# Gated linear attention in a two-layer hybrid block: the second head pair's projections get buffers of their own and are written ahead of its decays, and two modulation groups are written behind both pairs

## The chip, the cores and the metric

The kernel runs on one core of a Trainium2 chip. The metric is device time in microseconds (us) of one execution, median of three runs. Engines: PE is TensorE (matrix products), DVE is VectorE, ACT is ScalarE, POOL is GpSimd, SP is the engine whose queue issues the DMA transfers. PSUM is the small memory that PE writes to, here eight banks of 128 x 512 floats.

## The reference, cut to what matters

Two layers of a transformer block over 256 latent and 256 context tokens of width 1024. Each layer is modulated by six rows that come from a timestep vector (adaLN), has three parallel token mixers (grouped attention, gated linear attention, neighbourhood attention) and a mixture of experts. The part at hand is the gated linear attention (GLA) with 4 heads, which the kernel takes as 2 pairs of heads, and the modulation's product.

```
mod = silu(c) @ w_mod + b_mod              # 6 rows of 1024; a "group" here is 2 of the 6
z = h @ w_in + b_in                        # q, k (64 a head), v, r (128 a head), a (gate rank 16)
log_g = log_sigmoid(a @ w_gate + b_gate) / 16          # one for each direction: the decays
# per head and direction, over the tokens:
S_t = diag(exp(log_g_t)) S_{t-1} + k_t^T v_t
o_t = q_t S_t
o = rms_norm(o_forward + o_backward) * norm_g * silu(r)
```

## The kernel before

**Order of the work.** The program is written as plain Python that traces one instruction after the other. A scheduler then orders each engine's instructions by the order of tracing, by when it reckons that their inputs are ready, and by when buffers come free. What it decides is a fixed list for each engine: on the chip each engine works its list off in order, and an instruction that waits holds up all that stand behind it on its engine. The same holds for the transfers on SP's queue.

**One pair (`gla_pair`, L636).** `gla_decay` makes the decays: two small products z (L619), then on ACT and DVE absolute value, exponential, logarithm and running sums into the tile gc (C in the code). `projT` (L384) projects q and k, transposed, into the PSUM tiles pT, from which they are copied into the tile qTkT; `projM` (L393) projects V and the gate r of the four 128-token tiles into four PSUM tiles pM, from which V, r and rn are made. Then comes a chain. EK and EQ are the keys and queries times their decays. In two halves kET (PE transpose), kE (copy), dS (PE, one product a chunk) and a copy of dS. Eight levels of block products G (PE), each of which needs YX, made on DVE, POOL and ACT, and each of which is copied by mask into Sd on DVE; then Sd is copied to S on POOL. Then o (PE) for each token tile and each head of the pair, the RMS norm of o on ACT and DVE, and oT (PE transposes) with `put_o`, which casts oT to o0 on ACT and subtracts on DVE. In layer 0 a pair has four token tiles, in layer 1 two, as the context's output isn't needed there.

**Projections.** A matrix product in full precision is three products of parts (`mm3`: high by high, low by high, high by low; L380 to L382). So each weight piece of 128 x 1024 floats is loaded into a tile of the pool raw (4 buffers, 512 KB each) and split into whi (ACT, L291) and wlo (DVE, L292), which have 3 buffers each. A pair takes six pieces: one for q, one for k, four for V and r. One piece of q or k is 24 products, one of V and r is 24 too (6 for each of the four token tiles): 144 in all.

**Modulation (`modulation`, L471).** One group is 16 weight tiles (wmod) of 512 KB, which come from the pool raw as well, and two products of PE by each of them (L495), which the trace records as four. All 16 add up in one PSUM tile (mod), which is copied (L500) and transposed (modT). Layer 0 does group 1 behind pair 0 and group 2 behind pair 1; layer 1 does group 1 in its opening, with other buffers, and group 2 behind pair 1.

**PSUM.** The eight banks go by two names of four each. pT, pM, z, mod, modT and aT share one four; kET, dS, G, o and oT share the other.

**Pools.** g4 (10 buffers of 4 KB a partition in layer 0) holds ge, gc, qTkT, V, rn, EQ, EK, dS and S of a pair; o4 has 8 buffers, of which the output o0 of this mixer takes four.

Of the kernel before, what the change touches and what calls it, by code (L numbers as in the profile page):

```python
# [249 lines left out]
class _Prog:  # L250
# [385 lines left out]
    def gla_pair(self, l, pair, T):  # L636
        nc, mm = self.nc, self.nc.tensor.matmul
        nq = 128 * T
        C, end = self.gla_decay(pair)
        p = self.projT(l, ("Bq", pair), nq)  # L640
        qk = self.t([128, 2, 512], "g4", name="qTkT")
        qT, kT = qk[:, 0], qk[:, 1]
        nc.vector.tensor_scalar(qT[:, :nq], p[:, :nq], self.bt[:, BT["Bq", pair]:BT["Bq", pair] + 1], 0.125, op0=ALU.add, op1=ALU.mult)
        p = self.projT(l, ("Bk", pair), 512)
        nc.scalar.activation(kT, p, AF.Identity, bias=self.bt[:, BT["Bk", pair]:BT["Bk", pair] + 1])  # L645
        brow = self.bias_row(l, 768 + 512 * pair, 512)
        V = self.t([128, 4, 256], "g4", name="V")
        rn = self.t([128, 4, 256], "g4", name="rn")
        ps = self.projM(l, [("Bvr", pair, i) for i in range(4)], 2, 512, range(4), {t: 256 for t in range(T, 4)})
        for t in range(4):  # L650
            nc.vector.tensor_tensor(V[:, t], ps[t][:, :256], brow[:, :256], op=ALU.add)
            if t < T:
                r, th = self.t([128, 256], "u1", name="r"), self.t([128, 256], "u1", name="th")
                nc.vector.tensor_tensor(r, ps[t][:, 256:], brow[:, 256:], op=ALU.add)
                nc.scalar.activation(th, r, AF.Tanh, scale=0.5)
                nc.vector.scalar_tensor_tensor(r, th, 1.0, r, op0=ALU.add, op1=ALU.mult)
                nc.gpsimd.tensor_tensor(rn[:, t].rearrange("p (h e) -> p h e", h=2), r.rearrange("p (h e) -> p h e", h=2),
                                        self.gn[:, None, :].to_broadcast([128, 2, 128]), op=ALU.mult)

        F, B = C[:, 0], C[:, 1]  # L660
        EQ, EK = self.t([128, 2, 512], "g4", name="EQ"), self.t([128, 2, 512], "g4", name="EK")
# [15 lines left out]
        for i in (1, 0):  # L677
# [8 lines left out]
            for t in range(2):  # L686
                for d in range(2):
                    o = 256 * t + 128 * d
                    for h in range(2):
                        mm(pd[64 * h:64 * h + 64, o:o + 128], kE[:, t, d, 64 * h:64 * h + 64], V[:, 2 * i + t, 128 * h:128 * h + 128],  # L690
                           start=True, stop=True)
# [58 lines left out]
        for t in range(T):  # L750
            ts = slice(128 * t, 128 * t + 128)
            for h in range(2):
                hs = slice(64 * h, 64 * h + 64)
                inter = [(0, Sf), (1, Sb)]
                inter = [(i, s[t]) for i, s in inter if t in s]
                mm(pos[h][:, ts], S[:, t, h], V[:, t, 128 * h:128 * h + 128], start=True, stop=not inter)
                for n, (i, s) in enumerate(inter):
# [79 lines left out]
    def attention(self, l, T):  # L837
        nc, mm = self.nc, self.nc.tensor.matmul
        brow = self.bias_row(l, 0, 768)
        V = self.t([128, 4, 128], "u2", name="AV")  # L840
        kTs = self.t([128, 2, 512], "g4", F32R, "kTs")
# [3 lines left out]
        for t in range(4):  # L845
            z = self.t([128, 256], "u1", name="zkv")
            nc.vector.tensor_tensor(z, ps[t][:, :256], brow[:, 512:768], op=ALU.add)
            nc.gpsimd.tensor_copy(V[:, t], z[:, 128:])
            o = self.norm_rope(l, z[:, :128], 2, 1, t)
# [35 lines left out]
        def scores(qT, kv, pair):  # L885
            def emit(o, i, ks):
                for h in range(2):
                    q = qT[i][:, 2 * pair + h]
                    mm(o[h], q, kTs[:, kv, ks], start=True, stop=False)
                    mm(o[h], q, kTl[:, kv, ks], start=False, stop=True)  # L890
            return emit

        units = []
        for lat in ((True, False) if T == 4 else (True,)):
            qT = {}
            for pair in range(4):
                kv = pair // 2
                vs = slice(64 * kv, 64 * kv + 64)
                units.append(dict(lat=lat, prep=[lambda i=i, q=qT, t=i if lat else i + 2: q.__setitem__(i, prep(t)) for i in range(2)] if pair == 0 else [],
                                  scores=scores(qT, kv, pair), v=lambda k, h, vs=vs: V[:, k, vs], nb=None, out=(1, pair)))  # L900
        self.attend(units)
# [713 lines left out]
    def run(self):  # L1615
        nc, a = self.nc, self.a
        self.md, self.mT, self.mT2, self.nraw = {}, {}, {}, {}
        self.setup()
        self.rp = self.ctx.enter_context(self.tc.tile_pool(name="rp", bufs=1))
        self.x2 = [self.dr.tile([128, 1024], F32, name=f"x2_{t}") for t in range(2)]  # L1620
        src = [a["x"][0:128], a["x"][128:256], a["cx"][0:128], a["cx"][128:256]]
        xs = None
        for l in range(NL):
            T = 4 if l == 0 else 2
            if l == 0:
                left, right = self.mixers(0)
                xs = []
                for t in range(4):
                    x = self.t([128, 1024], "o4", name="x")
                    nc.sync.dma_start(x, src[t])  # L1630
                    xs.append(x)
                self.vectors(l)
                self.setup2()
                self.modulation(0, [0], ["h4"] * 8 + ["y4"] * 4 + ["raw"] * 4)
            self.norm_T(l, xs)
            if l:
                self.modulation(1, [1], "o4", "b2", "tmod")
            if l:
                self.vectors(l)
            self.oT, self.y = {}, []  # L1640
            self.gla_gates(l)
            self.open_o(0)
            for p in range(2):
                self.gla_pair(l, p, T)
                if l == 0 or p == 1:
                    self.modulation(l, [1 + p])
            self.held, self.nw, self.spare = {}, 0, []
            us = groups(l)[0][0]
            self.load(l, us, 0, range(4), most=PRE[l], after=self.aT)
            self.open_o(1)  # L1650
            self.attention(l, T)
            self.merge(l, 0, T)
            self.open_o(2)
            self.neighbourhood(l, T)
            self.merge(l, 1, T)
            self.merge(l, 2, T)
            self.out_norm(l, T, src if l == 0 else self.x2)
            left.close()
            left = self.open("eg", "left", [("ew", 6)])
            if l == 0:  # L1660
                self.modulation(1, [0], "ew")
            self.load(l, us, 0, range(4), most=6)
            self.route(l, T)
            if not LAST[l]:
                self.h2_done(l, T - 1)
            if l:

                self.spare = [[self.t([128, 1024], ("whi", "wlo")[v] if tag == "wx" else tag, name="ew") for v in range(2)] for tag in ("raw", "h4", "h4", "wx")]
            right.close()
            right = self.open("ep", "right", [("ewb", RNG[l]), ("e8", 2), ("g2", T // 2), ("oh", 2), ("o1", 2), ("e2", NE2[l]), *([("c2", NC2[l])] if l else []), ("ct", NCT[l]), ("row", 2)])  # L1670
            self.experts(l, T)
            if l:
                lgb = self.final_loads(l)
            self.overflow(l, T)
            if l == 0:
                right.close()
                left.close()
                self.pre.close()
                left, right = self.mixers(1)
                lgb = self.final_loads(l)  # L1680
            xs = self.final_norm(l, T, lgb)
        right.close()
        left.close()
        self.pre.close()
# [27 lines left out]
```

## Time and profile before

| what | value |
|---|---|
| median of three runs | 2152.49 us (2150.43 to 2153.63) |
| the profiled execution | 2150.77 us, span 2148.9 us |
| PE busy | 1973.0 us, 92% of the span |
| DVE, ACT, POOL busy | 45%, 26%, 13% |
| mean granted clock of PE | .969 |
| moved by DMA | 562.41 MB, mean 262 GB/s |

The span is the stretch from the first to the last instruction of the profiled execution; the 1.9 us beside it are start and end. Stages on the time axis: layer 0 opens until 52 us, its two GLA pairs take until about 216, its other mixers until about 700, its experts until about 1190 (at 370 to 420 GB/s). Layer 1's GLA pairs lie between about 1245 and 1370, its experts from about 1650 to the end. Numbers of times below are us from the start of the span.

### The profile page before, as it was taken

The page shows a single profiled execution, that of the slowest core. Times are in us where ns is not written, and L with a number is a line of the kernel's source. Part 1 is how long each engine was busy: PE and PEld are TensorE (multiplying, and loading weights), DVE is VectorE, ACT ScalarE, POOL GpSimd, SP SyncE. Part 2 cuts the span into 40 slices and gives each one's busy share as a digit, 9 for nine tenths or more (in the row PEclk, how much of TensorE's full clock was granted, in tenths as well). Part 3 has the DMA queues.
Part 4 walks back from the last instruction along what each step waited for, and adds up shares of the span by engine and source line. Part 5 has one row for each costly group of instructions (what it writes and reads, how often), then busy time and mean ns, then how long its engine had stood idle before and what let it go on. Part 6 is the DMA issues. An engine that isn't in the chain of part 4 may idle for free. (4 is left out here: it accounts for less than half of the span.)

```text
span 2148.9 us, 28075 instructions
## 1 busy us (share of the span) xinstructions
PE 1973.0 (92%) x10749; PEld 1179.0 (55%) x10749; DVE 964.7 (45%) x2236; ACT 561.5 (26%) x992; POOL 277.5 (13%) x268
## 2 busy tenths in 40 slices
PE   6999999999998898989899598999996999999995
PEld 2676777767885353445253176887795433333331
DVE  4676765554487131222022766776658222221113
ACT  3453344443333000000010254444452111100000
POOL 1322100011100010111011222100020001000000
PEclk9999999999999999999999798999997999999998
DMA  8436222333328999999998723642466999999995
GB/s 300 160 118 220 69 69 70 94 99 120 99 91 321 400 420 420 372 385 420 420 369 367 276 84 116 197 127 85 140 210 253 401 421 422 422 422 422 421 422 224
DMA packets 113987, 562.41 MB, mean 262 GB/s; under 512 B 13302, under 2 KB 14838, under 8 KB 72120
## 3 DMA queue, kind: packets, MB, share of 16 engines
q1 hardware_dynamic: 113272, 558.85, 67.7%
q8 instruction: 87, 1.43, 0.3%
q10 hardware_dynamic: 576, 1.70, 0.2%
q14 instruction: 52, 0.43, 0.1%
HBM read 557.36 MB, written 3.15 MB: 261 GB/s over the span
## 5 line engine op out<-in xcount | busy, mean ns | idle before, releaser
L1507 PE MATMUL h<-ew,XT 128*64 128x512 f32 (+2 forms) x2048 | 479.0, 616 | 39.6 <-DMA ew<-in_ew_dram 39.5
L1507 PEld LDWEIGHTS h<-ew,XT 128*64 128x64 f32 (+2 forms) x2048 | 147.3, 136 | 325.7 <-issue 251.0
L1415 PE MATMUL Y<-ew,aT 128*64 128x512 f32 (+2 forms) x1024 | 250.4, 598 | 10.2 <-DMA ew<-in_ew_dram 7.8
L292 DVE TENSOR_TENSOR wlo<-raw,whi 128x1024 fp32r<-128x1024 f32 (+1 forms) x140 | 179.1, 1279 | 138.0 <-ACT whi L291 136.9
L1433 POOL TENSOR_TENSOR x<-x,ct 128x512 f32<-128x512 f32 x82 | 104.9, 1306 | 996.9 <-DVE ct L1432 873.7
L380 PE MATMUL pT<-hThi,whi 128*128 128x512 f32 (+1 forms) x576 | 204.0, 354 | 2.2 <-DVE zq L869 1.4
L291 ACT CAST whi<-raw 128x1024 fp32r<-128x1024 f32 (+1 forms) x140 | 145.4, 1039 | 223.4 <-PE pT L381 123.8
L382 PE MATMUL pT<-hThi,wlo 128*128 128x512 f32 (+1 forms) x576 | 203.2, 353 | 0.2 <-DVE wlo L292 0.2
L381 PE MATMUL pT<-hTlo,whi 128*128 128x512 f32 (+1 forms) x576 | 202.9, 352 | 0.0
L1404 DVE SCALAR_TENSOR_TENSOR act<-h,s,sl 128x512 f32<-128x512 f32 x30 | 22.5, 751 | 317.6 <-PE h L1507 263.9
L806 ACT CAST Yh<-Y 128x512 fp32r<-128x512 f32 x60 | 35.2, 586 | 467.7 <-PE Y L1415 467.7
L1415 PEld LDWEIGHTS Y<-ew,aT 128*64 128x64 f32 (+2 forms) x1024 | 75.5, 133 | 149.2 <-issue 123.8
L807 DVE TENSOR_TENSOR Yl<-Y,Yh 128x512 fp32r<-128x512 f32 x60 | 41.4, 690 | 252.8 <-ACT Yh L806 249.7
L380 PEld LDWEIGHTS pT<-hThi,whi 128*128 128x128 f32 x576 | 110.7, 192 | 23.8 <-issue 6.0
L382 PEld LDWEIGHTS pT<-hThi,wlo 128*128 128x128 f32 x576 | 110.7, 192 | 16.1 <-issue 2.6
L381 PEld LDWEIGHTS pT<-hTlo,whi 128*128 128x128 f32 x576 | 110.7, 192 | 14.3 <-issue 1.9
L380 PE MATMUL pM<-whi,hThi 128*128 128x512 f32 (+1 forms) x304 | 110.7, 369 | 3.6 <-ACT qTkT L645 1.9
L381 PE MATMUL pM<-wlo,hThi 128*128 128x512 f32 (+1 forms) x304 | 110.9, 365 | 0.0
L382 PE MATMUL pM<-whi,hTlo 128*128 128x512 f32 (+1 forms) x304 | 110.1, 364 | 0.0
L495 PE MATMUL mod<-wmod,sT 128*32 128x512 f32 x320 | 75.2, 636 | 22.5 <-DVE s L341 14.1
L1408 ACT COPY aT<-aT 128x512 f32<-128x512 f32 x30 | 17.6, 585 | 294.4 <-PE aT L1407 294.4
L1384 PE MATMUL XT<-OH,h2hi 128*128 128x256 f32 x352 | 88.6, 289 | 0.2 <-DVE OH L1362 0.2
(364 smaller groups left out, 3088.5 us busy)
## 6 DMA issues: line engine op xcount, KB each, us to landing
ew<-in_ew_dram SPq DMA_DIRECT2D x326, 1024.0 KB, 13.6
raw<-in_w_dram SPq DMA_DIRECT2D x145, 512.0 KB, 3.7
ew<-in_ew_dram SPq DMA_DIRECT2D x116, 512.0 KB, 13.5
wmod<-in_wmod_dram SPq DMA_DIRECT2D x96, 512.0 KB, 6.4
nb<-in_nb_dram SPq DMA_DIRECT2D x32, 256.0 KB, 3.8
g<-md SPq DMA_DIRECT2D x12, 256.0 KB, 7.3
row<-in_ln_dram SPq DMA_DIRECT2D x4, 512.0 KB, 5.3
lgb<-in_ln_dram SPq DMA_DIRECT2D x4, 512.0 KB, 12.2
```

The source lines that it names most:

```text
L291: self.nc.scalar.copy(hi, src)
L292: (eng or self.nc.vector).tensor_tensor(lo, src, hi.bitcast(F32), op=ALU.subtract)
L380: mm(out, lh, rh, start=start, stop=False)
L381: mm(out, lh, rl, start=False, stop=False)
L382: mm(out, ll, rh, start=False, stop=stop)
L495: nc.tensor.matmul(p[32 * j:32 * j + 32, :], self.sT[:, k, :], raws[j // 2][:, 512 * (j % 2):512 * (j % 2) + 512], start=k == 0, stop=k == 7)
L806: self.nc.scalar.copy(hi, src)
L807: self.nc.vector.tensor_tensor(lo, src, hi.bitcast(F32), op=ALU.subtract)
L1384: mm(p[:, w * j:w * j + w], self.h2s[t][part][:, 128 * k:128 * k + 128], OH[:, t], start=t == 0 and part == 0, stop=t == T - 1 and part == 1)
L1415: mm(y[m * i:m * i + m, :], aT[:, 128 * f + m * i:128 * f + m * i + m], w2(f, n, i), start=f == 0, stop=f == 3)
L1433: (nc.vector if last and n else nc.gpsimd).tensor_tensor(self.x1[t][:, ns], self.x1[t][:, ns], tmp, op=ALU.add)
L1507: mm(h[m * i:m * i + m, :], XTs[dp][:, k, 128 * pr + m * i:128 * pr + m * i + m], w[i, 2 * q + k // 4][k % 4], start=k == 0, stop=k == 7)
```

## The change

In `gla_pair` the call of `gla_decay` stays first for pair 0, and is written behind the projections (q, k, V, r) for pair 1. The tiles qTkT, V and rn of pair 1 come from the pool o4 in place of g4. In `run` the modulation of group 1 and of group 2 in layer 0 are both written behind the two pairs; in layer 1 group 2 stays where it was. No instruction is added or taken away.

```diff
     def gla_pair(self, l, pair, T):
...
-        C, end = self.gla_decay(pair)
+        if pair == 0:
+            C, end = self.gla_decay(pair)
         p = self.projT(l, ("Bq", pair), nq)
-        qk = self.t([128, 2, 512], "g4", name="qTkT")
+
+        own = ("g4", "o4")[pair]
+        qk = self.t([128, 2, 512], own, name="qTkT")
...
-        V = self.t([128, 4, 256], "g4", name="V")
-        rn = self.t([128, 4, 256], "g4", name="rn")
+        V = self.t([128, 4, 256], own, name="V")
+        rn = self.t([128, 4, 256], own, name="rn")
...
+        if pair:
+            C, end = self.gla_decay(pair)
...
             for p in range(2):
                 self.gla_pair(l, p, T)
-                if l == 0 or p == 1:
-                    self.modulation(l, [1 + p])
+            self.modulation(l, [2] if l else [1, 2])
```

How the scheduled lists change is seen at three places. Numbers behind a tile's name tell one buffer's use from another.

**PE, layer 0, at the end of pair 0's projections.** pM_87 is the last of pair 0's projections; mod_167 is group 1 of the modulation; kET_112 to dS_117 are pair 0's chain. Before:

```order
L381 MATMUL pM_87_484<-wlo_99_578,hThi_45_274 128x512
L382 MATMUL pM_87_484<-whi_98_577,hTlo_49_278 128x512
L495 MATMUL mod_167_1024<-wmod_168_1025,sT_139 32x512 x2
L495 MATMUL mod_167_1024<-wmod_169_1026,sT_139 32x512 x2
L495 MATMUL mod_167_1024<-wmod_170_1033,sT_139 32x512 x2
L495 MATMUL mod_167_1024<-wmod_171_1034,sT_139 32x512 x2
L682 MATMUL kET_112_647<-cst_72,EK_109_634 128x128 x4
L690 MATMUL dS_114_654<-V_82_479,kE_113_652 64x128 x8
L682 MATMUL kET_115_664<-cst_72,EK_109_634 128x128 x4
L495 MATMUL mod_167_1024<-wmod_172_1041,sT_139 32x512 x2
L495 MATMUL mod_167_1024<-wmod_173_1042,sT_139 32x512 x2
L690 MATMUL dS_117_671<-V_82_479,kE_116_669 64x128 x8
```

Of the change (pT_170 and pT_175 are pair 1's q and k, pM_179 to pM_182 its four tiles of V and r, z_205 and z_206 its decays, mod_267 is group 1):

```order
L382 MATMUL pM_87_484<-whi_98_577,hTlo_49_278 128x512
L380 MATMUL pT_170_1030<-hThi_42_271,whi_168_1026 128x512
...
L382 MATMUL pM_180_1094<-whi_190_1159,hTlo_48_277 128x512
L695 MATMUL dS_117_671<-V_82_479,kE_116_669 64x128 x8
L708 MATMUL G_120_683<-qTkT_76_443 64x64
...
L780 MATMUL oT_166_1017<-cst_72,o_160_988 128x128
L380 MATMUL pM_181_1095<-whi_184_1099,hThi_42_271 128x512
...
L382 MATMUL pM_182_1096<-whi_193_1189,hTlo_49_278 128x512
L619 MATMUL z_205_1247<-aT_62_382,wg_7_118 128x512
L619 MATMUL z_206_1250<-aT_62_382,wg_7_118 128x512
L495 MATMUL mod_267_1659<-wmod_268_1660,sT_139 32x512 x2
```

At the first dots stand 81 products of pair 1's projections together with kET_112, dS_114 and kET_115; at the second pair 0's 128 G products and all of its o and oT, with three more products of pair 1's projections among the G; at the third the rest of pM_181 and pM_182 and the last piece's products for all four tiles, 60 in all with the rows shown. Group 1's 32 products, which stood among pair 0's chain, stand behind all of it. In layer 1 the order is alike, with 84 products of pair 1's projections ahead of pair 0's last dS, 60 behind its oT, and then z and group 2; there nine of group 2's 16 tiles stand ahead of pair 1's kET, four among its kET and dS, the last three among its G, and 28 of the 64 G products of pair 1, which stood ahead of the last tile or beside it before, stand behind it.

**DVE, layer 0.** This is the end of pair 0's output (o_160 is its last normalised tile, o0_65 the subtraction of `put_o`) and the start of pair 1's values (qTkT_171 from pT_170, wlo_194 from the last weight piece, V_177 from pM_179). Of the change:

```order
L775 SCALAR_TENSOR_TENSOR o_160_988<-o_160_988,s_163_996,rn_83_480 128x128 x2
L793 TENSOR_TENSOR o0_65_387<-oT_165_1010,o0_63_385 128x512
L646 TENSOR_SCALAR qTkT_171_1055<-pT_170_1030,bt_96 128x512
L793 TENSOR_TENSOR o0_65_387<-oT_166_1017,o0_63_385 128x512
L292 TENSOR_TENSOR wlo_194_1190<-raw_192_1187,whi_193_1189 128x1024
L654 TENSOR_TENSOR V_177_1091<-pM_179_1093,brow_176_1089 128x256
```

Before, the same copy of pT stood within pair 0's norm, with two of its steps ahead of it and most of them behind it:

```order
L633 TENSOR_TENSOR s_191_1124<-gc_188_1104,ge_187_1103 128x4
L767 TENSOR_SCALAR s_144_911<-s_141_904 128x2
L643 TENSOR_SCALAR qTkT_196_1157<-pT_195_1132,bt_96 128x512
L276 TENSOR_SCALAR s_145_913<-s_144_911 128x2
L284 TENSOR_TENSOR s_146_914<-s_145_913 128x2
```

So the copy that empties pT moved from the first tile's norm to behind the last one's. In layer 1 the copy of pT has the same new place, between the two subtractions of `put_o`.

**SP, layer 0, the queue of transfers.** ew_307 is an expert's weight that is loaded early, brow a row of biases. Before:

```order
L592 DMA brow_81_477<-in_bm_dram 128x512
L1464 DMA ew_307_1816<-in_ew_dram 128x2048
L493 DMA wmod_168_1025<-in_wmod_dram 128x1024
L493 DMA wmod_169_1026<-in_wmod_dram 128x1024
L493 DMA wmod_170_1033<-in_wmod_dram 128x1024
L493 DMA wmod_171_1034<-in_wmod_dram 128x1024
```

Of the change:

```order
L1469 DMA ew_307_1816<-in_ew_dram 128x2048
L373 DMA raw_167_1024<-in_w_dram 128x1024
L373 DMA raw_172_1057<-in_w_dram 128x1024
L373 DMA raw_183_1097<-in_w_dram 128x1024
L373 DMA raw_186_1127<-in_w_dram 128x1024
L373 DMA raw_189_1157<-in_w_dram 128x1024
L373 DMA raw_192_1187<-in_w_dram 128x1024
L493 DMA wmod_268_1660<-in_wmod_dram 128x1024
L493 DMA wmod_269_1661<-in_wmod_dram 128x1024
L493 DMA wmod_270_1668<-in_wmod_dram 128x1024
L592 DMA brow_176_1089<-in_bm_dram 128x512
L493 DMA wmod_271_1669<-in_wmod_dram 128x1024
```

The pool raw has four buffers, so wmod_271 takes that of raw_192, and wmod_272, which stands next, that of wmod_268. The six pieces of pair 1 moved ahead of all 32 wmod tiles.

## Rows read from the trace of the kernel before

**Rows 1.** Page, part 1: busy us, share of the span, instructions.

```profile
PE 1973.0 (92%) x10749; PEld 1179.0 (55%) x10749; DVE 964.7 (45%) x2236; ACT 561.5 (26%) x992; POOL 277.5 (13%) x268
```

**Rows 2.** Waits of PE, 50 to 250 us: sum, count, longest.

```profile
PE mod L495 <- DMA wmod<-in_wmod_dram: 5.7, 5, 2.7
```

**Rows 3.** Timeline of PE, layer 0's GLA: start, duration, instruction, count, idle before.

```profile
86.61 0.39 PE L382 MATMUL pM<-whi,hTlo 128*128 128x512 f32 x1
86.92 1.92 PE L495 MATMUL mod<-wmod,sT 128*32 128x512 f32 x16
89.63 0.66 PE L682 MATMUL kET<-cst,EK 128*128 128x128 f32 x4 [0.79 <-DVE EK L673]
90.97 1.09 PE L690 MATMUL dS<-V,kE 128*64 128x128 f32 x16 [0.68 <-ACT kE L684]
...
112.11 1.05 PE L495 MATMUL mod<-wmod,sT 128*32 128x512 f32 x4
...
121.73 0.38 PE L756 MATMUL o<-V,S 128*128 128x128 f32 x2
122.05 0.71 PE L758 MATMUL o<-st,EQ 64*128 64x128 f32 x4
...
187.01 1.05 PE L495 MATMUL mod<-wmod,sT 128*32 128x512 f32 x4
```

**Rows 4.** The same timeline, first of pair 0's V and r products.

```profile
71.06 0.50 PE L380 MATMUL pM<-whi,hThi 128*128 128x512 f32 x1 [1.86 <-ACT qTkT L645]
```

**Rows 5.** Timeline of the other engines in layer 1's GLA.

```profile
1264.03 0.15 DVE L633 TENSOR_TENSOR s<-gc,ge 128x4 f32<-128x4 f32 x1
1292.05 0.58 ACT L692 COPY dS<-dS 128x512 f32<-128x512 f32 x1 [1.19 <-PE dS L690]
1300.79 0.84 POOL L740 COPY S<-Sd 64x256 f32<-64x256 f32 x2 [4.25 <-DVE Sd L732]
1319.83 0.16 DVE L276 TENSOR_SCALAR s<-s 128x2 int32<-128x2 int32 x1
1321.79 0.61 DVE L770 SCALAR_TENSOR_TENSOR o<-o,s,rn 128x128 f32<-128x128 f32 x2
```

**Rows 6.** Timeline of DVE, POOL and ACT, layer 0's GLA.

```profile
95.88 0.35 DVE L746 SCALAR_TENSOR_TENSOR st<-st,s,dS 128x128 f32<-128x128 f32 x1 [2.72 <-ACT dS L692]
107.57 0.77 DVE L732 COPY_PREDICATED Sd<-c_mask,G 128x256 f32<-128x256 uint8 x2
114.39 3.00 POOL L740 COPY S<-Sd 64x512 f32<-64x512 f32 x2 [10.01 <-DVE Sd L732]
123.30 0.19 ACT L765 ACTIVATION_READ_ACCUMULATOR sq<-o 128x1 f32 x1
214.53 1.07 ACT L787 CAST o<-oT 128x512 fp32r<-128x512 f32 x2 [3.76 <-PE oT L775]
```

**Rows 7.** Timeline of PE in layer 1's GLA.

```profile
1247.30 3.07 PE L619 MATMUL z<-aT,wg 33*128 33x512 f32 x4 [1.48 <-ACT aT L608]
1277.62 1.98 PE L619 MATMUL z<-aT,wg 33*128 33x512 f32 x4
1301.33 0.79 PE L380 MATMUL pM<-whi,hThi 128*128 128x512 f32 x1
1307.50 0.39 PE L382 MATMUL pM<-whi,hTlo 128*128 128x512 f32 x1
1349.06 1.05 PE L495 MATMUL mod<-wmod,sT 128*32 128x512 f32 x4
```

**Rows 8.** Windows, layer 1: PE, PEld, DVE, ACT, POOL busy; granted clock; DMA share; GB/s.

```profile
1295.00:1300.00 5.00, 2.76 (x61) 2.08 (x52) 4.37 (x15) 1.26 (x2) 1.22 (x2) 0.58 0.01 3
1300.00:1305.00 5.00, 4.82 (x25) 3.90 (x26) 1.01 (x5) 4.00 (x9) 0.79 (x2) 0.50 0.00 0
```

**Rows 9.** Timeline of PE in the opening: two tiles of the modulation's group 0.

```profile
27.93 1.05 PE L495 MATMUL mod<-wmod,sT 128*32 128x512 f32 x4 [0.22 <-DMA wmod<-in_wmod_dram]
29.14 1.05 PE L495 MATMUL mod<-wmod,sT 128*32 128x512 f32 x4 [0.15 <-DMA wmod<-in_wmod_dram]
```

## The prediction

> **What bounds the kernel now.** Read the page's first part first: PE works 92% of the span [rows 1], so a stretch of the GLA costs what PE has to do in it, unless something leaves PE idle. Then the waits of PE between 50 and 250 us: the weight tiles of the modulation hold it five times, for 5.7 us together [rows 2]. That is little, and the timeline of PE says why [rows 3]: when pair 0's last projection ends (86.61 + .39 = 87.0 us) four tiles of the modulation lie ready and run without a gap, then come kET and dS with gaps under .8 us, and the chain of pair 0 goes on with the modulation's products in its gaps. So the kernel before has two things to do at once in both pairs: a chain that runs through DVE, ACT and POOL with short products between, and PE work that doesn't depend on it. In pair 0 the modulation's group 1 is that cover, and its transfers run while the chain does; then pair 1's projections cover pair 0's o; then group 2 covers pair 1's chain. The last wmod tile ends at 187.01 + 1.05 = 188.06. What the change does is read by following one list of each engine through that stretch, in either layer, as its order stands now, with the durations of the rows.
>
> **What the change moves.** No instruction is added. In layer 0 pair 0's chain loses the modulation as cover and gets the first 81 of pair 1's 144 projection products; the other 60 (and z, which now stands behind them) can't start under the chain. Their PSUM tiles are two of the four of their name, and two of those hold pT of q and k until they are copied; these copies now stand behind pair 0's whole output on DVE (the lists show it) and on ACT. And all 32 wmod tiles come behind that, through four buffers which the weight pieces use as well.
>
> **Layer 0, step by step.** A projection product takes (86.61 - 71.06) / 68 = .229 us [rows 3, 4]: the first of the tile's group starts at 71.06, 68 products later the last one does. From 87.0: 81 of them 18.5, twice kET at .66 and twice dS at 1.09 [rows 3] 3.5: 109.0. The copy of dS .58, from layer 1's row of the same shape [rows 5]: 109.6. Then the chain. From its first state product to the end of a Sd copy near its end it took 95.88 to 108.34, 12.5 us [rows 6], on a DVE that was seldom idle; I add two pairs of Sd copies that were still to come (1.5) and the copy of Sd to S on POOL (3.0): 17.0, so o starts at 126.6. (To the end of POOL's copy the trace took 117.39 - 95.88 = 21.5, with G waiting behind modulation products that now are gone.) Eight heads' o, (122.05 + .71) - 121.73 = 1.03 each [rows 3]: 134.8. ACT's copy and square of the last one, 123.49 - 122.76 = .73 [rows 3, 6]: 135.5. The norm on DVE, 1322.40 - 1319.83 = 2.57 [rows 5]: 138.1. The casts of oT 1.07 [rows 6] and then the copy of pT, .58 as for dS: 139.8. Now 60 products, 13.7, and 2.3 because PE starts slow: after a like stall in layer 1, 17 products took 6.17 us (1301.33 to 1307.50) where 17 x .229 is 3.89 [rows 7], at a granted clock of .50, the lower of its two levels (1.2 GHz), after 5 us with scattered work at .58 [rows 8]. That ends at 155.8, z (1.98 [rows 7]) at 157.7.
>
> Only four wmod tiles can lie ready then, because SP's queue stands at the fifth, whose buffer waits for PE: 28 tiles come at the pace of the transfers. That pace lies between 1.21 us (27.93 to 29.14, with 16 buffers and nothing else to do [rows 9]) and 2.03 us (88.84 to 113.16 for twelve tiles, four buffers, chain between [rows 3]). Neither is this case; I take 1.7, nearer to the second, since it is the same four buffers and each waits for PE, for SP's issue and for the transfer in turn. 28 x 1.7 = 47.6: the last tile ends at 205.3, against 188.06: +17.3. But five of pair 1's eight heads' o now stand ahead of it, which stood behind: -5.2. **Layer 0: +12.1.** Bounds: at 2.03 a tile, +21.3. At 1.21 the tiles end at 191.6, and pair 1's chain sets the end: 157.7, decays 15.1 (below), kET and dS 3.5, copy .6, two tiles 1.1, chain 17.0, five heads 5.2 make 200.2 against 193.2: +7.0.
>
> The Trainium skill's page "DMA: Bandwidth & Descriptors", section Bandwidth, says to batch transfers to 1 MiB or more and has 341 GB/s at 1 MB and 425 at 16 MB; by these a tile of 512 KB would take 1.23 to 1.54 us, an estimate, and layer 0 would cost between +7.0 and some +8. The row with 16 buffers agrees with the quick end, the row with four does not; I go by the rows.
>
> **Layer 1.** Pair 1's z started at 1277.62 [rows 7]; the same place now starts its q. 84 products 19.2, kET and dS 3.5, copy .58: 1300.9. The chain with two token tiles: 1292.63 to 1301.63, 9.0 us [rows 5]: 1309.9. Four heads 4.1, ACT .73, norm 2.57, casts of half width .53, copy .58: 1318.4. 60 products, 36 and 12 of them of half width, 8.2, and a slow start 2.3: 1328.9. z 1.98: 1330.9. From z's end to the end of the decays took 1247.30 + 3.07 to 1264.18, 13.8 us [rows 5, 7], and EK's product another 1.3: kET at 1346.0; nine tiles of the modulation fit into that. kET, dS 3.5 and four tiles' products 1.9: 1351.4; three more tiles at 1.7: 1356.5. Before, the last ended at 1349.06 + 1.05 = 1350.11 [rows 7]: +6.4. Then 28 products of G stand behind it, with two levels' Sd copies (1.5) and the copy of S (.84), and the next stage's weight pieces queue behind the last wmod tiles (two transfers, 2.4); between 0 and 4.8, I take 2.4, since next stage's products stand between them as cover. **Layer 1: +8.8.** Bounds: +2.6 (tiles at 1.21, no slow start, nothing behind) to +12.2 (tiles at 2.03, all 4.8).
>
> **Sum.** +20.9, bounds +9.6 and +33.5. Later stages give nothing back by what I see: they start from PE's end of this one, and the experts' weights can be fetched ahead only as far as their buffers go. Against the profiled execution, 2150.8 us, that is 2171.7; the median of the runs is 1.7 higher: **2173.4**.
>
> **Rivals.** *The projections do fill the chain (faster).* If PE had enough of them ready from 87.0 until pair 0's o ends, the modulation's 5.7 us of waits [rows 2] and layer 1's slow start of 2.3 [rows 7, 8] would go: 2150.8 - 8.0, median 2144.5. For it: 144 products are 33 us, more than the chain's 17. Against: 81 are spent before the last dS, and 60 wait for PSUM. It decides where the copy of pT comes: if it ended before pair 0's chain does (126.6) instead of at 139.8, the 60 products lay under o and its norm. The lists put it behind the norm.
>
> The Trainium skill's page "PSUM — Partial Sum Buffer", section "Summary: rules for kernel authors", says "Evacuate promptly"; the trace of before, where pT was copied within the norm of the first o, does not show the opposite.
>
> *Much slower: the clock stays low.* After 5 us of thin work PE ran at .50 [rows 8]. If it is at that level through the exposed stretches, 12 heads' o in both layers take another 12.3 us, and two further starts 2.3 each: +38, median 2190. For it: stretches of 20 us with nothing but G and o. Against: o's part is short, and DVE and POOL, which set the chain, don't slow down.
>
> *No difference.* All terms at their low ends give +9.6; it would need the chain, 17.0, to shrink to about 11, because DVE no longer works on weight pieces among it.
>
> **Chances.** The forecast's own range, 2162 to 2186 (bounds on the median), .66. Much slower .20. No difference .06. Faster .08. The runs before spread over 3.2 us; 0.2% (4.3 us) is about what a measurement of this kernel can tell from no change. So faster by over 0.2% .08, within .06, slower .86. The range holds the forecast's and most of the much slower case and of the spread: 2159 to 2191.
>
> **What would show it.** In the changed profile: the first pM product behind oT_166 near 140 us with a wait for the copy of qTkT (DVE or ACT) of 5 us or more behind it; DMA nearly idle from about 110 us to about 157 us; wmod waits of PE far above 5.7 us (by 1.7 - .5 a tile, some 20 to 30 us); z of pair 1 near 158; the last tile of group 2 near 205; in layer 1 z near 1329 plus the shift of layer 0, and the last tile 6 us later than that shift. A clock near .5 in the 20 us ahead of pM_181 and longer than 4 us behind it would speak for the much slower case. I'm wrong in the mechanism if pM_181 starts before 130 or if wmod tiles arrive while pair 0's chain runs; wrong in a size if the tile pace isn't between 1.21 and 2.03.

## Result and the profile after

The changed kernel takes 2202.22 us (median of four runs, 2197.25 to 2206.51), the kernel before 2151.46 us in its four (2149.6 to 2153.63): the ratio is 1.0235 with a 95% interval of 1.021 to 1.0259. The change costs 51 us, where 21 were forecast; the range ended at 2191, 39 above before's median. The page of the changed kernel, part 1 (beside [rows 1]), and the waits of PE between 50 and 250 us, the longest (beside [rows 2]):

```profile
PE 1990.5 (91%) x10749; PEld 1189.7 (54%) x10749; DVE 961.7 (44%) x2236; ACT 562.6 (26%) x992; POOL 277.6 (13%) x268
```

```profile
PE dS L695 <- ACT kE L689: 7.6, 1, 7.6
PE mod L495 <- DMA wmod<-in_wmod_dram: 7.1, 10, 2.8
PE G L708 <- DVE Sd L737: 4.8, 5, 2.2
PE pM L380 <- ACT qTkT L648: 3.4, 2, 1.9
PE oT L780 <- DVE o L775: 2.5, 2, 1.4
PE modT L503 <- DVE mg L500: 2.3, 1, 2.3
```

The work is the same to the instruction, yet PE is busy 17.5 us longer. Where that is shows in windows over the two GLA stages, from the end of pair 0's projections (layer 0) or pair 0's z (layer 1) to the first qT product of the attention. Before, and then the changed kernel (columns as in [rows 8]):

```profile
87.00:256.00 169.00, 156.19 (x1252) 109.94 (x1253) 120.18 (x332) 66.48 (x134) 47.25 (x57) 0.98 0.48 159
1247.00:1413.60 166.60, 157.83 (x1183) 127.38 (x1184) 115.81 (x312) 77.94 (x138) 36.99 (x61) 0.94 0.45 141
```

```profile
88.00:285.10 197.10, 168.36 (x1254) 117.17 (x1253) 114.32 (x330) 64.92 (x132) 48.17 (x57) 0.87 0.39 131
1276.70:1462.50 185.80, 162.33 (x1186) 129.19 (x1187) 116.23 (x311) 78.52 (x137) 35.74 (x61) 0.92 0.40 126
```

Layer 0's stage is 28.1 us longer: 15.9 us more in which PE idles (28.7 against 12.8) and 12.2 us more of the same products, at a mean clock of .87 in place of .98. Layer 1's is 19.2 us longer (19.5 from the exact start of z, as in the table below): 14.7 idle, 4.5 busy. The rest, some 3 us, is spread over the stages between. The timeline of PE in the changed kernel shows layer 0's steps (beside [rows 3]):

```profile
125.25 0.80 PE L761 MATMUL o<-V,S 128*128 128x128 f32 x2 [0.29 <-POOL S L745]
125.97 1.22 PE L763 MATMUL o<-st,EQ 64*128 64x128 f32 x4
...
144.88 0.80 PE L380 MATMUL pM<-whi,hThi 128*128 128x512 f32 x1 [1.49 <-ACT qTkT L648]
...
161.12 1.98 PE L619 MATMUL z<-aT,wg 33*128 33x512 f32 x4
163.04 1.92 PE L495 MATMUL mod<-wmod,sT 128*32 128x512 f32 x16
167.79 4.21 PE L495 MATMUL mod<-wmod,sT 128*32 128x512 f32 x12 [2.83 <-DMA wmod<-in_wmod_dram]
...
176.02 0.66 PE L687 MATMUL kET<-cst,EK 128*128 128x128 f32 x4 [1.36 <-DVE EK L678]
176.61 1.06 PE L495 MATMUL mod<-wmod,sT 128*32 128x512 f32 x8
185.30 1.11 PE L695 MATMUL dS<-V,kE 128*64 128x128 f32 x7 [7.63 <-ACT kE L689]
...
225.07 1.05 PE L495 MATMUL mod<-wmod,sT 128*32 128x512 f32 x4 [0.20 <-DMA wmod<-in_wmod_dram]
```

Read it against the forecast's steps, whose times stand in brackets: o starts at 125.25 (126.6), the 60 bare products at 144.88 (139.8), z ends at 163.1 (157.7), the last tile at 226.1 (205.3). Windows of the same kernel show what lies in the gaps: PE at .50 through pair 0's o and norm, and at 180 us a stretch in which PE does nothing at all while POOL and ACT work.

```profile
115.00:120.00 5.00, 2.59 (x48) 2.38 (x48) 5.00 (x9) 1.71 (x2) 1.54 (x1) 0.59 0.00 0
120.00:125.00 5.00, 4.18 (x84) 3.65 (x80) 2.67 (x7) 0.73 (x2) 1.02 (x2) 0.50 0.02 5
...
140.00:145.00 5.00, 1.59 (x5) 0.85 (x5) 3.79 (x18) 1.66 (x3) 0.00 (x0) 0.50 0.00 0
...
180.00:185.00 5.00, 0.00 (x0) 0.00 (x0) 3.31 (x3) 2.90 (x4) 4.27 (x4) 0.58 0.42 170
```

### The profile page after: what moved, and what is told of

Same layout as the page of the kernel before. It is cut to its first block, busy times and chain, and to the rows that moved or that the text cites. A ratio compares the mean times of both kernels' runs of the same rounds, so it can differ in the third digit from the quotient of the medians.

```text
span 2199.3 us, 28079 instructions
## 1 busy us (share of the span) xinstructions
PE 1990.5 (91%) x10749; PEld 1189.7 (54%) x10749; DVE 961.7 (44%) x2236; ACT 562.6 (26%) x992; POOL 277.6 (13%) x268
## 5 line engine op out<-in xcount | busy, mean ns | idle before, releaser
L381 PEld LDWEIGHTS pT<-hTlo,whi 128*128 128x128 f32 x576 | 109.8, 191 | 14.1 <-issue 1.9
L495 PE MATMUL mod<-wmod,sT 128*32 128x512 f32 x320 | 77.2, 690 | 28.1 <-DVE s L344 14.8
## 6 DMA issues: line engine op xcount, KB each, us to landing
lgb<-in_ln_dram SPq DMA_DIRECT2D x4, 512.0 KB, 12.2
```

What stands on the lines that cost most here:

```text
L381: mm(out, lh, rl, start=False, stop=False)
L495: nc.tensor.matmul(p[32 * j:32 * j + 32, :], self.sT[:, k, :], raws[j // 2][:, 512 * (j % 2):512 * (j % 2) + 512], start=k == 0, stop=k == 7)
```

## The experiments

The change has three parts, which can be undone one by one: **M**, group 1 behind both pairs (layer 0 only); **B**, own buffers from o4; **D**, pair 1's decays behind its projections. Six runs are the other corners; four have B with its tiles first written early; the rest test single costs. The table gives the parts that a kernel has, its median, the ratio to the kernel before run beside it with its interval, and how much longer than before's the two stages are in the trace: from the start of pair 0's z to the first qT product, layer 0 (206.0 us before) and layer 1 (166.3 us before).

| run | parts | us | ratio (95%) | layer 0 | layer 1 |
|---|---|---|---|---|---|
| changed kernel | M B D | 2202.2 | 1.0235 (1.021 to 1.0259) | +28.1 | +19.5 |
| x8 | M | 2171.3 | 1.0068 (1.0048 to 1.0087) | +15.8 | -0.2 |
| x9 | B | 2164.6 | 1.0045 (1.0028 to 1.0062) | +5.0 | +5.5 |
| x10 | D | 2176.3 | 1.0098 (1.008 to 1.0117) | +9.8 | +8.9 |
| x1 | M D | 2175.4 | 1.0122 (1.0087 to 1.0157) | +11.9 | +7.4 |
| x2 | B D | 2193.4 | 1.0203 (1.0175 to 1.0232) | +14.1 | +19.3 |
| x3 | M B | 2185.4 | 1.0156 (1.0133 to 1.0179) | +22.3 | +5.4 |
| x4 | M B D, first write early | 2179.2 | 1.0128 (1.0102 to 1.0154) | +18.7 | +9.4 |
| x5 | M B, first write early | 2183.8 | 1.016 (1.0138 to 1.0181) | +20.6 | +6.9 |
| x6 | B D, first write early | 2176.4 | 1.0107 (1.0087 to 1.0128) | +10.1 | +7.3 |
| x7 | B, first write early | 2168.6 | 1.0069 (1.0049 to 1.009) | +1.5 | +15.8 |
| x11 | M B D, POOL relieved | 2198.1 | 1.0204 (1.0183 to 1.0225) | +25.0 | +16.0 |
| x12 | M B D, chain filled | 2222.6 | 1.031 (1.0266 to 1.0353) | +40.1 | +24.5 |

A stage's figure comes from one traced execution. Layer 1's order hardly depends on M, so pairs of kernels that differ by M alone show how far such a figure can be trusted: they agree in layer 1 within 2.1 us, but for x5 and x7 (+6.9 and +15.8, see x7).

**x1, own buffers undone.**

```diff
-        own = ("g4", "o4")[pair]
+        own = "g4"
```

> The changed kernel with one part undone: pair 1's qTkT, V and rn come from g4 again; the order of decays and projections and the place of the modulation stay changed. The scheduled list then has the copy of pT ahead of pair 0's norm, and all of pair 1's projections under pair 0's o. Theory U (the buffers make the copy of pT wait for pair 0's output, so 60 products lie bare): layer 0 gets back the stretch from 125 to 145 us less eight heads at full speed (8) and the slow start (2.3), some -14, and layer 1 some -10: about 2178 us. Theory D (what costs is pair 1's decays behind its projections): both layers keep their z to kET stretches of 13 and 15 us and the dS wait of 7.6 us: 2195 to 2205. Theory M (the modulation's tiles): layer 1 as in the changed kernel, layer 0 a few us less: 2195 to 2205.

2175.4 us: theory U. Both layers get back 12 to 16 us; z of pair 1 starts at 149.2 in place of 161.1. The copy of pT on DVE starts at 124.6, in the changed kernel at 144.4. Why a buffer moves a copy is read from the lists: the scheduler hands out o4's buffers in the order in which the program first writes them, and pair 0's output tiles come first, so the copy of pT stands behind `put_o`. x4 bears it out: there the copy starts at 93.8.

**x2, group 1 back behind pair 0.**

```diff
-            self.modulation(l, [2] if l else [1, 2])
+                if l == 0 or p == 1:
+                    self.modulation(l, [1 + p])
```

> The changed kernel with one part undone: group 1 of layer 0 stands behind pair 0 again; own buffers and the order of decays and projections stay changed. Layer 1's list is that of the changed kernel, so its loss of some 21 us must stay under each theory. Theory M (16 tiles lost their cover in layer 0): layer 0 back by 20 to 28 us: 2174 to 2182. Theory D (decays): layer 0 keeps z to kET and the dS wait, at least 13 us of its 28: 2187 to 2195. Theory U: pair 0's output still stands ahead of the copy of pT, 60 products still stand behind it, but the chain ahead is covered by tiles: 2187 to 2197.

2193.4: layer 1 is unchanged as it must be, and layer 0 gets back 14 of 28. Half of layer 0's loss, and more than half of all, isn't the tiles.

**x3, decays back ahead of the projections.**

```diff
-        if pair == 0:
-            C, end = self.gla_decay(pair)
+        C, end = self.gla_decay(pair)
...
-        if pair:
-            C, end = self.gla_decay(pair)
```

> The changed kernel with one part undone: pair 1's decays are written ahead of its projections again; own buffers and the modulation behind both pairs stay. Theory D: in layer 0 the stretch from z's end to dS (163.1 to 185.3, 22 us) falls to some 3, less what the tiles did in it (7 tiles, 9 us): -10 to -16; in layer 1 1360.5 to 1378.5 likewise -8 to -14, and the G behind the last tile go back: about 2175. Theory U: the bare stretch of pair 0's output stays in both layers, so no less than 2170, and theory M (layer 1 isn't touched by it) says at least 2185.

2185.4, where theory D expected about 2175: layer 1 gets back 14.1, layer 0 only 5.7 where 10 to 16 were expected. With the decays early, layer 0 still has 32 tiles behind 60 bare products.

**x4, first writes early.** B's tiles are taken and touched ahead of the pairs, all else as changed.

```diff
...
+            self.own = [self.t([128, 2, 512], "o4", name="qTkT"), self.t([128, 4, 256], "o4", name="V"), self.t([128, 4, 256], "o4", name="rn")]
+            for t in self.own:
+                nc.gpsimd.memset(t[:, 0, 0:1], 0.0)
             self.open_o(0)
```

> The changed kernel with pair 1's three tiles taken before the output tiles are, and one column of each set to zero by POOL ahead of the pairs; same pool, same buffers, decays and modulation as changed. In the list the copy of pT goes from behind pair 0's whole output to the middle of pair 0's G, and all 144 projection products of pair 1 lie among pair 0's chain. Theory U: the 16 us of bare products per layer go, and o runs at full clock: about -22 us in layer 0 and -12 in layer 1 against the changed kernel, 2165 to 2172, and z of pair 1 starts at 138 to 145 us. Theory D/M (decays and tiles behind it set the time): z earlier only lets the 28 tiles start earlier, which also gains; but if the tiles' pace of 2 us rules, the last tile ends near 200 to 205. If the buffers themselves cost (reuse, ports) and not the place of the copy: no change, 2197 to 2207.

2179.2: the mechanism holds, the size was too large. Here is the whole aim of the change reached: 144 products lie in pair 0's chain, the clock holds (windows of x4; the first two answer to those of the changed kernel above), z starts at 138.70. But of these 22.4 us layer 0 keeps 9.3: later, in pair 1's o with its tiles, PE stands at .50 for 20 us and more.

```profile
115.00:120.00 5.00, 5.00 (x82) 4.02 (x81) 4.11 (x8) 1.06 (x1) 1.06 (x2) 1.00 0.00 0
120.00:125.00 5.00, 5.00 (x81) 3.99 (x81) 3.78 (x8) 1.06 (x1) 0.14 (x1) 1.00 0.02 3
...
200.00:205.00 5.00, 5.00 (x15) 2.61 (x14) 0.41 (x3) 1.34 (x6) 0.00 (x0) 0.50 0.52 169
205.00:210.00 5.00, 5.00 (x15) 2.24 (x13) 1.82 (x15) 1.34 (x6) 0.00 (x0) 0.50 0.35 101
```

**x5, x6 and x7: the same with D undone, with M undone, and with both** (the diffs of x3 and x2 on top of that of x4).

> As the run with the first writes ahead, with pair 1's decays written ahead of its projections again; modulation behind both pairs. Theory D: z to kET and dS leave the path in both layers: another -8 to -12 in layer 1 and some -5 in layer 0, since there 28 tiles at 1.2 to 2 us still come behind the projections: 2155 to 2162. Theory M then is what is left: layer 0 +10 to +15, layer 1 at 0 or below.

> As the run with the first writes ahead, with group 1 of layer 0 behind pair 0 again; decays behind the projections. Layer 1 as in the run with the first writes ahead. In layer 0 the list has group 1 among pair 0's chain and the projections among o, but z and the decays stay bare: 2160 to 2170 by theory D (13 to 20 us in layer 0); 2152 to 2158 if only the modulation's place and the copy of pT mattered.

> The kernel before with nothing but own buffers for pair 1 (o4), taken early and first written ahead of the pairs; decays ahead and group 1 behind pair 0 as before. Layer 0's list is nearly that of before; in layer 1 the copy of pT comes within pair 0's chain, and its products start at the first G. Theory U expects a small gain, in layer 1 alone, from G's waits (4.2 us) and the slow start (2.3): 2145 to 2150. If own buffers cost by themselves: 2155 or more.

x5 missed: undoing D gives nothing (layer 0 +20.6 against +18.7); the clock, which x4 held in pair 0's chain and o, stands at .50 there from 120 to 135. x6 lies above what was expected, with 10.1 left in layer 0. x7 missed on the other side: layer 0 is back (+1.5), but layer 1, where a small gain was expected, is +15.8. There pair 0's chain took the products that before lay under its o, oT and pair 1's kET, and those now run bare. But x5, whose order in layer 1 is nearly the same, does so too and is at +6.9, so this is less than half of it. The other 8.8 us lie between the second kET of pair 1 and the last tile, 29.5 us against 20.7 in x5: PE waits 1.55 us for a tile at 1360.53 and then stands near .50 through pair 1's o. Windows of x7, layer 1's stage (mean clock .88 against .94 before) and pair 1's o, and of x5, the same place:

```profile
1253.40:1435.50 182.10, 169.41 (x1183) 135.42 (x1184) 116.63 (x312) 78.17 (x137) 37.28 (x61) 0.88 0.40 129
1361.50:1371.50 10.00, 10.00 (x34) 5.77 (x32) 1.31 (x8) 2.91 (x13) 0.00 (x0) 0.53 0.58 195
```

```profile
1375.00:1385.00 10.00, 9.93 (x79) 4.75 (x73) 2.96 (x14) 3.63 (x16) 0.79 (x2) 1.00 0.97 333
```

x7's six runs lie between 2159.3 and 2172.5 us, and the traced one took 2172.4. What the shorter ones did at this place isn't known.

**x8, x9 and x10: one part alone**, the other two undone as in x1 to x3.

> The kernel before with one part alone: group 1 of layer 0 is written behind both pairs; decays, projections and buffers as before. Layer 1's list is that of before: 0 there by each theory. Layer 0: pair 0's G have no cover, 28 tiles of 512 KB come behind the projections. Theory M: +10 to +18 in layer 0, 2162 to 2170 in all. If the tiles only cost together with the late copy and the late decays: within 4 us of before.

> The kernel before with one part alone: pair 1's qTkT, V and rn come from o4. In the list 60 products of pair 1 then stand behind pair 0's oT in both layers, the decays ahead of them. Theory U: pair 0's norm and the slow start come bare in both layers, +4 to +7 in layer 0 and +8 to +12 in layer 1: 2164 to 2171. If the buffers cost only with the decays late: within 4 us of before.

> The kernel before with one part alone: pair 1's decays are written behind its projections; buffers and modulation as before. Theory D: z to kET and dS come bare: +10 to +16 in layer 0 and +6 to +9 in layer 1: 2168 to 2177. If the decays' 13 us hide behind the 9 tiles ahead of kET: 2156 to 2162.

By their totals all three fall in their theory's place, x8 a little above it, as its other stages are 7 us longer in the trace. M costs layer 0 15.8 and layer 1 nothing, B some 5 in each (in layer 1 8 to 12 were expected), D 9 to 10 in each. Alone they sum to 30.5 in layer 0 (28.1 together) and 14.2 in layer 1 (19.5 together). They don't simply add: M beside D costs 2.1 more than D alone, B beside D in layer 1 10.4 where B alone costs 5.5.

**x11, two subtractions of pair 1's YX moved from POOL to DVE.**

```diff
-            nc.gpsimd.tensor_tensor(x[:, :, 1], g[:, :, 1], bm, op=ALU.subtract)
-            nc.gpsimd.tensor_tensor(y[:, :, 0], bm, g[:, :, 0], op=ALU.subtract)
+            (nc.vector if pair else nc.gpsimd).tensor_tensor(x[:, :, 1], g[:, :, 1], bm, op=ALU.subtract)
+            (nc.vector if pair else nc.gpsimd).tensor_tensor(y[:, :, 0], bm, g[:, :, 0], op=ALU.subtract)
```

> The changed kernel with pair 1's two subtractions for YX that POOL did (L729, L730) on DVE; the list of PE stays nearly the same. In the changed kernel the first dS of pair 1 in layer 0 waits 7.6 us for the copy kE on ACT, which stands behind four YX that POOL finishes late (its first one took 3.62 us beside DVE's 0.42 us ones, .73 elsewhere). Theory P (POOL is slowed beside DVE): kE comes 4 to 5 us earlier, 2196 to 2199; 8 subtractions more on DVE at .41 cost less than they free. If DVE's own work sets the time: no change or slower, 2201 to 2206.

2198.1 is theory P's place and 4 us below the changed kernel, but the runs of the two overlap (2195.8 to 2202.8, and 2197.3 to 2206.5), so the time alone doesn't show a gain. The trace shows the step: the wait of dS for kE falls from 7.6 to 3.7 us (waits of PE in x11, 160 to 190 us), and the stages are 3.0 and 3.4 us shorter.

```profile
PE dS L695 <- ACT kE L689: 3.7, 1, 3.7
```

**x12, pair 0's chain filled with products without use**, so that PE doesn't wait.

```diff
+            if pair == 0:
+                for i in range(8):
+                    x0 = self.hT(0, i)
+                    mm(pg[i % 2][:, c0:c0 + 256], x0[:, :128], x0[:, :256], start=True, stop=True)
             blocks(pg, YX[:, 1], YX[:, 0], lv == 6, c0)
```

> The changed kernel with 56 products more per layer that serve no output: ahead of the G of each of pair 0's seven YX levels, 8 products of 128x256 go into the PSUM columns that this level's G overwrite. PE is busy while it waits for YX. Theory C (part of the loss is the clock, which stood at .50 from about 117 to 150 us): o takes 1.03 us a head instead of 1.7 and the 60 products behind start at full speed; -5 and -2.3 in layer 0, -3.4 and -2.3 in layer 1, less some 2 us by which the chain gets longer: 2190 to 2195. If only idle engines count: 2202 to 2207, as PE does more.

2222.6, against theory C's number, and no proof against the clock: it fell in spite of the filling, after one wait of 2.0 us for a Sd copy at 120.4, and the filler products then ran at half speed too (windows of x12). Three of its runs took 2222 to 2223 us, one 2207.6. How much of the changed kernel's loss a full clock alone would give back stays untested.

```profile
115.00:120.00 5.00, 4.90 (x71) 4.01 (x73) 5.00 (x10) 2.12 (x2) 4.31 (x6) 1.00 0.00 0
120.00:125.00 5.00, 2.96 (x46) 2.48 (x41) 4.56 (x8) 1.06 (x1) 0.33 (x1) 0.77 0.02 3
125.00:130.00 5.00, 5.00 (x42) 4.15 (x41) 0.00 (x0) 0.00 (x0) 0.00 (x0) 0.50 0.00 0
```

**x13 and x14, half of the tiles' transfers in layer 0**, in the changed kernel and in that before (as many products).

```diff
-                    raws = [self.t([128, 1024], tag if isinstance(tag, str) else tag[2 * k + h], name="wmod") for h in range(2)]
-                for h in range(2):
+                    raws = [self.t([128, 1024], tag if isinstance(tag, str) else tag[2 * k + h], name="wmod") for h in range(1 if tag == "raw" and l == 0 else 2)]
+                    raws = raws * (3 - len(raws))
+                for h in range(1 if tag == "raw" and l == 0 else 2):
                     nc.sync.dma_start(raws[h], self.a["wmod"][l, g, k, h])
```

One tile is taken and loaded where two were, and used for both, so the four buffers of raw reach twice as far; the scheduler then puts the tiles' products earlier in PE's list (in the changed kernel the last of them ahead of pair 1's last G, not among its o). The modulation's values change and with them the experts' work, so whole times (2304.2 and 2254.3 us) say nothing; layer 0's stage does, since the routing comes behind it.

> The changed kernel with half of the transfers of layer 0's groups 1 and 2: the first of each two tiles is loaded and used for both, so the modulation's values are other ones; the products are as many. Theory T (the tiles' transfers set the stretch from z to the last tile): 16 tiles fewer at 1.7 to 2.2 us, -20 to -30: 2172 to 2182. Theory L (pair 1's chain of 37 us and PE's list set it, the transfers only fill the waits): -3 to -12: 2190 to 2199, as decays, dS wait and chain remain.

> The kernel before with half of the transfers of layer 0's groups 1 and 2, as in the other run. It had 5.7 us of waits of PE for these tiles. If the transfers lie under the chains there: -2 to +4 us, 2148 to 2156. If they bound it too: -8 us or more, 2143 or less.

The changed kernel's stage is 17.4 us longer than before's full one, so it gains 10.7, theory L's place; the kernel before gains 8.6 as well, though its transfers seemed hidden. At half the transfers the two kernels still lie 26.0 us apart, at full 28.1. So the transfers cost time in both kernels, but they don't make the difference between them.

## Why the prediction was wrong

**The direction held, and the first half of the mechanism.** The copy of pT stands behind pair 0's output in both layers, 60 products and z behind it, PE waits 1.49 us for it at 144.88. SP's queue does nothing for wmod between 101.97 and 155.41, as its timeline in the changed kernel shows:

```profile
101.60 0.33 SPq L493 DMA_DIRECT2D wmod<-in_wmod_dram  x1
101.97 0.43 SPq L592 DMA_DIRECT2D brow<-in_bm_dram  x1
155.41 0.33 SPq L493 DMA_DIRECT2D wmod<-in_wmod_dram  x1
```

Three of the forecast's own signs came out against it. PE's wait for the copy of pT is 1.49 us, not 5 or more. Its waits for wmod between 50 and 250 us are 7.1 us, not 20 to 30 more than 5.7. And the pace of the 28 tiles is 63.0 / 28 = 2.25 us, outside 1.21 to 2.03, which it had called wrong in a size. The sign of the much slower case came: .50 from 120 to 145.

The rule that the prediction quoted from the Trainium skill ("PSUM — Partial Sum Buffer", section "Summary: rules for kernel authors", "Evacuate promptly") agrees with the runs where pair 1's decays stand behind its projections: with the copy early x1 takes 27 us less than the changed kernel, x4 23 us less, and x6 17 us less than x2. With the decays ahead an early copy gives nothing: x5 takes 2183.8 and x3 2185.4, x7 2168.6 and x9 2164.6.

**Layer 0 was forecast at +12.1 and came to +28.1.** *"Eight heads' o, 1.03 each"*: they took 13.6 us, as PE stood at .50: +5.3. That is the part of the much slower rival which came true, and the forecast had priced the low clock only as slow starts of 2.3. With the chain 2 us shorter and the norm 1 longer, z ended 4.4 late, counted from the same start. *"28 tiles come at the pace of the transfers"* is the step that failed: from z's end to the last tile it took 63.0 us, not 47.6. The window of that stretch and PE's waits in it:

```profile
163.10:226.12 63.02, 44.60 (x448) 16.96 (x447) 29.57 (x60) 21.46 (x35) 22.80 (x22) 0.86 0.76 266
```

```profile
PE dS L695 <- ACT kE L689: 7.6, 1, 7.6
PE mod L495 <- DMA wmod<-in_wmod_dram: 7.1, 10, 2.8
PE modT L503 <- DVE mg L500: 2.3, 1, 2.3
PE kET L687 <- DVE EK L678: 1.4, 1, 1.4
```

A DMA share of .76 over 63.0 us is 47.9 us, near the 47.6 forecast (the next stage's weight pieces, from 220 us on, are in it). What the forecast left out is the time in which the transfers stood. Tiles and pair 1's chain stand on one list of PE, and each waits for the other: while PE waited 7.63 us for kE no tile was used up, so in the end none was fetched (DMA share .42 from 180 to 185, .02 from 185 to 190). Of PE's waits in the stretch 7.1 us are for tiles and 11.3 for the chain. Its products for tiles take 30.5 us of its busy time, .95 a tile, where four ready tiles took 1.92 (163.04) and a tile that comes alone 1.05 (225.07); so the tiles' pace costs more than the waits for them say. Taking the later end of two streams, as the forecast did, was wrong here; the waits of both add. With half the transfers (x13) the stretch is 36.6 us, but the stage gains only 10.7, as pair 1's chain then ends behind the tiles. And the chain itself had been taken too short: 22 us from kET to o, out of a stretch of pair 0's, while the trace of before has pair 1's first kET at 162.1 and its first o at 195.3, 33 us; in the changed kernel it is 42 (176.0 to 218.0). Behind the last tile 3.8 us more came back than the 5.2 expected.

**Layer 1 was forecast at +8.8 and came to +19.5.** To the last tile the forecast was right, +6.4 against 7.7, in part by luck: counted from the same start, pair 0's o began 4.0 us sooner than forecast, but took 3.5 longer at .50, and the norm behind it 1.2 longer. *"28 products of G behind it ... between 0 and 4.8, I take 2.4"* is mis-sized: from the last tile to the attention's first qT product the changed kernel needs 75.3 us, the one before 63.5: 11.8. The count was wrong too: 28 of the 64 G products stand behind modT, and behind the last tile itself stand 40 (80 of the 128 records). Windows from the last tile to the first kTs product, the changed kernel and then before:

```profile
1387.20:1421.50 34.30, 31.09 (x244) 26.42 (x245) 21.85 (x84) 13.11 (x30) 3.27 (x9) 0.95 0.41 131
```

```profile
1350.10:1374.90 24.80, 24.80 (x167) 22.35 (x166) 18.80 (x70) 11.04 (x24) 1.70 (x5) 1.00 0.58 190
```

Of the 9.5 us between them 6.3 are PE's own work, which the forecast left out altogether: 3.6 are the G that now stand there (77 records more in all), the rest is the same products taking longer, in part at a clock of .66 from 1415 to 1420. 3.2 are waits, for wlo, zkv and mg. The other 2.3 come later, up to the qT product.

**Of the rivals**, "the projections do fill the chain" is refuted twice: in the changed kernel they don't, and in x4, where they do, the time is still 1.0128 of before. "No difference" fell with the sizes. The range, taken from bounds of single terms, was too narrow: they had nothing for PE's waits for pair 1's chain and for PE's own work behind layer 1's last tile, and the low clock during o was priced in a rival, not on top of them.

## What to carry to other kernels

When a change moves cover from one chain to another, follow both: here x4, which covered pair 0's chain in full, got back 9.3 of layer 0's 28.1 us, and pair 1's o then ran at .50. None of the eleven other arrangements (x1 to x11) beat the kernel before. Where independent work and a chain share an engine's in-order list, don't take the later of the two ends for granted: ask what each does while the engine waits for the other, and price the stretch a second time at the lower clock. A buffer can move an instruction: read in the scheduled list where the copy that empties PSUM stands before counting on what comes behind it.

## What the runs showed of the hardware that was not expected

POOL's subtraction of 128 x 256 floats took .73 us in pair 0's chain and 3.62 in pair 1's, where DVE ran the same shape back to back. Timelines of the changed kernel, POOL, DVE and ACT:

```profile
111.01 0.73 POOL L729 TENSOR_TENSOR YX<-gc 128x256 f32<-128x256 f32 x1 [13.57 <-PE G L708]
...
171.19 3.62 POOL L729 TENSOR_TENSOR YX<-gc 128x256 f32<-128x256 f32 x1 [0.48 <-DVE gc L631]
...
183.08 1.04 POOL L672 TENSOR_TENSOR EQ<-s,gc 128x512 f32<-128x512 f32 x1
```

```profile
171.55 0.43 DVE L727 TENSOR_TENSOR YX<-gc 128x256 f32<-128x256 f32 x1
171.90 0.42 DVE L728 TENSOR_TENSOR YX<-gc 128x256 f32<-128x256 f32 x1
```

```profile
184.15 0.63 ACT L674 ACTIVATE EQ<-EQ 128x512 f32<-128x512 f32 x1
184.68 0.57 ACT L689 COPY kE<-kET 128x512 f32<-128x512 f32 x1
```

POOL comes to EQ only at 183.08, ACT does EQ and then kE, which had its input since 176.7, and PE's dS waits. In the kernel before, pair 1's first such subtraction took 2.98 us too (at 126.26); what is new is that PE waits for what comes behind it. The Trainium skill, "SBUF — State Buffer", section "SBUF: two separate sides", has a DVE instruction with two inputs in SBUF and a GpSimd instruction that reads SBUF share a pair of ports, which one of them holds for its whole instruction while the other stands still. These rows agree with it, as POOL's 3.62 us end .5 us behind the last of DVE's eight; no run here shows that the ports are the reason, and x11 shows only what moving the work gains.

In layer 0 the clock fell to .50 between 105 and 130 us in the kernels that have no tiles in pair 0's chain (the changed one, x1, x3, x5, x8, x11 and x12), and stayed at 1.00 from 95 to 135 in those that have them (before, x2, x6, x7, x9 and x10) and in x4, whose chain is filled with projections. It stayed low while PE was almost fully busy again: .50 in x12's window from 125 to 130 us, with PE busy for all 5 us of it, and in x4's from 200 to 210. "TensorE: Matmul & The Clock Gate", section "HAM oscillation — how this bites in real kernels", of the Trainium skill tells of waits for transfers in a loop of products that bring the clock down. The fall in x12 agrees in kind, but it came behind one wait of 2.0 us for a copy on DVE, shorter than the page's waits.
